# A LoRA router softmax on one Trainium2 core: sixteen idle semaphore instructions leave the programs of VectorE and ScalarE

## The chip, the core and the metric

The kernel runs on one core of a Trainium2 chip. A core has a matrix engine (TensorE, in the profile PE for the products and PEld for the loading of weights), VectorE (DVE), ScalarE (ACT), GpSimd (POOL), SyncE (SP) and 16 DMA engines. Each engine runs a program of its own, in order, and the programs meet through semaphores: an instruction may wait until a semaphore has reached a value, and may change one when it is done. A `q` behind an engine's name in the profile is its sequencer, the part that waits, branches and issues.

The metric is device time in microseconds (us). A time is a median over several runs; a profile is one execution, and its span goes from the first to the last instruction that was recorded.

## What is computed

```python
def reference(x, router_weights):          # x: 16 x 512 x 1024, router_weights: 1024 x 8, fp32
    logits = np.matmul(x, router_weights)
    exp_logits = np.exp(logits - np.max(logits, axis=-1, keepdims=True))
    return (exp_logits / np.sum(exp_logits, axis=-1, keepdims=True)).astype(np.float32)
```

There are 8,192 rows of 1,024 numbers, and a softmax over 8 router logits for each. Nearly all the data is `x`: 32 MB that are read once.

## The kernel before

The 8,192 rows are dealt to the 128 partitions, 64 to each, so that the work falls into 64 tiles (`J = 64`, numbered `j`) of 128 rows. A tile is called a row here, as in the code.

**Loading.** SP loads rows 0 to 3 in fp32 in two transfers (line 138), and ScalarE casts them to bf16 (`cast`, lines 338 to 341). The other rows are loaded by GpSimd's queue, which casts on the way: 12 transfers of four rows, three of two, five of one, and the last row in three pieces (lines 172 to 187). All are issued early, and `x_all` holds every row, so no transfer ever waits for a buffer. SP turns each landing into counts of `s_in`, one for each row (lines 156 to 162).

**The work on a row.** TensorE waits for `s_in`, turns the eight 128x128 blocks of the row (`loop_turn`, transposes into the PSUM tiles `ptv` and `pts`), VectorE copies five of the turned blocks to SBUF (`dve_copy`, line 403) and ScalarE the other three (`act_copy`, line 355), and TensorE multiplies them with the router weights (`multiply`). There are two sets of these buffers, used by even and odd rows. Two products of a constant tile (`fill`) are done in each pass of TensorE's loop besides.

**Softmax.** For eight rows at a time (`G = 8`) VectorE takes the maximum, subtracts it, sums, takes the reciprocal and scales, and ScalarE does the exponential. These steps are strung between the copies of the rows that come next.

**The loops.** TensorE, VectorE and ScalarE each run a loop with a branch at its end. VectorE's program is: two casts while it starts, a semaphore count (line 397), two register moves (lines 462 and 463), four copies for rows 0 to 3, then the body `dve_rows` (lines 469 to 488), seven times, and `dve_done` for what is left. ScalarE's is: `cast(0)`, two copies, `cast(1)`, two copies, a register move, then the body `act_rows` (lines 368 to 376), seven times, and `act_done`. The body of VectorE's loop has 20 instructions and that of ScalarE's 13, the branch included. A body handles eight rows, so the seventh pass ends with row 59. Rows 60 to 63 are handled after the loops, and row 63 in its three pieces: a maximum, an exponential and a matmul of its own for each row (`low_alone`, `power_alone`), then one sum, reciprocal and scaling for the four, and the last output transfer (line 167).

**The idle instructions.** Two constants, `DVE_IDLE, ACT_IDLE = 5, 11` (line 53), say how often a semaphore `s_idle` is raised that nobody waits for. ScalarE does it 11 times in front of `cast(0)` (lines 357 and 358), VectorE 5 times between its count of `s_p` and its register moves (lines 398 and 399). They stand ahead of the loops, each once, and so the address of everything behind them in the same program depends on them.

## Time and profile before

| | us |
|---|---|
| median of 4 runs (86.56 to 86.7) | 86.62 |
| the profiled execution, its own time | 86.61 |
| its span, first to last instruction | 85.2 |
| VectorE busy, of the span | 39.5 (46%) |
| ScalarE busy | 38.0 (45%) |
| TensorE busy (products / weight loads) | 62.6 (74%) / 51.4 (60%) |
| the queue of GpSimd's transfers, share of 16 DMA engines over the span | 90.4% |
| mean granted TensorE clock, share of full speed | 0.987 |

The profile of one execution has a page (busy times, 40 slices of the span, DMA queues, the chain of work that ended last, groups of instructions by line) and a trace behind it that can be asked for single lines, for waits or for a stretch of time. "Idle" in front of a group is time in which its engine did nothing, and the arrow names what ended it. Time of an engine that waits for data is no loss in itself; what counts is what the chain that ended last went through. Semaphore, register and branch instructions aren't counted as busy, but the trace has a record of each.

### The profile page before, as it was taken

How to read it: one execution, taken by the hardware profiler on the slowest of the kernel's cores; microseconds unless marked ns; L12 is line 12 of the kernel's file. 1: busy time of each engine (PE TensorE's matmuls, PEld its weight loads, DVE VectorE, ACT ScalarE, POOL GpSimd, SP SyncE). 2: the span in 40 equal slices, each digit the busy share in tenths (PEclk: the TensorE clock that was granted, in tenths of full speed). 3: DMA queues.
4: the chain of work that ended last, by engine and by line, in shares of the span. 5: the costliest groups of instructions: out<-in, count | busy, mean ns of one | idle time of the engine just before them, and what ended most of it. 6: DMA issues, size and time to landing. Idle time of an engine off the chain costs nothing. (4 is left out here: it accounts for less than half of the span.)

```text
span 85.2 us, 2942 instructions
## 1 busy us (share of the span) xinstructions
PE 62.6 (74%) x1094; PEld 51.4 (60%) x1094; DVE 39.5 (46%) x114; ACT 38.0 (45%) x81; POOL 13.5 (16%) x30
## 2 busy tenths in 40 slices
PE   0053849999595986949596895959598699999760
PEld 0041747878474765838475673847476588777650
DVE  0020413685274452745266362736347257665662
ACT  0039682665254352535245253525336246546470
POOL 0489999800000000000000000000000000000000
PEclk9999999999999999999999999999999999999995
DMA  2899999999999999999999999999999999999920
GB/s 46 358 427 312 223 196 227 204 227 208 223 204 223 208 223 208 227 204 227 204 227 204 227 204 227 204 223 208 223 208 204 214 215 214 203 209 211 184 102 23
DMA packets 3904, 18.12 MB, mean 213 GB/s; under 512 B 568, under 2 KB 1080, under 8 KB 2112
## 3 DMA queue, kind: packets, MB, share of 16 engines
q0 software_dynamic: 3312, 15.73, 90.4%
q1 hardware_dynamic: 576, 2.36, 7.0%
q10 hardware_dynamic: 16, 0.03, 0.3%
HBM read 33.59 MB, written 0.26 MB: 397 GB/s over the span
## 5 line engine op out<-in xcount | busy, mean ns | idle before, releaser
L355 ACT COPY xTs<-pts 128x384 bf16<-128x384 bf16 x63 | 30.0, 477 | 37.4 <-PE pts L282 37.0
L403 DVE COPY xTv<-ptv 128x640 bf16<-128x640 bf16 x63 | 31.0, 492 | 33.0 <-PE ptv L282 30.4
L282 PE MATMUL ptv<-identity,x_all 128*128 128x128 bf16 x311 | 28.3, 222 | 13.9 <-PEq L218 12.5
L282 PEld LDWEIGHTS ptv<-identity,x_all 128*128 (+1 forms) x311 | 18.5, 98 | 15.2 <-issue 15.2
L282 PE MATMUL pts<-identity,x_all 128*128 128x128 bf16 x186 | 21.1, 224 | 0.0
L269 PEld LDWEIGHTS lg<-w_bf,xTv 128*128 128x128 bf16 x305 | 15.5, 97 | 7.4 <-issue 0.6
L269 PE MATMUL spare<-filler 128*128 128x512 bf16 x61 | 19.0, 393 | 0.5
L269 PE MATMUL lg<-w_bf,xTv 128*128 128x8 bf16 x305 | 16.6, 167 | 0.0
L282 PEld LDWEIGHTS pts<-identity,x_all 128*128 x186 | 13.5, 100 | 0.0
L269 PE MATMUL lg<-w_bf,xTs 128*128 128x8 bf16 x183 | 13.2, 166 | 0.0
L174 POOL DMA_DIRECT2D x_all<-in_x_dram x20 | 10.8, 602 | 2.8 <-POOLq L151 2.8
L269 PEld LDWEIGHTS lg<-w_bf,xTs 128*128 128x128 bf16 x183 | 8.9, 96 | 0.0
L269 PEld LDWEIGHTS spare<-filler 128*128 128x128 bf16 x61 | 4.3, 99 | 2.5 <-issue 2.5
L276 PE MATMUL lg<-ident,w 8*128 8x8 f32 x8 | 1.0, 251 | 5.3 <-PEq L274 5.3
L276 PEld LDWEIGHTS lg<-ident,w 8*128 8x128 f32 x8 | 0.9, 197 | 5.3 <-issue 5.3
L341 ACT CAST x_all<-x_f 128x1024 bf16<-128x1024 f32 x4 | 4.0, 1044 | 0.0
L423 DVE TENSOR_REDUCE mx<-lg 128x8 f32 x8 | 1.8, 225 | 4.4 <-DVEq L473 3.9
L341 ACT ACT_TABLE_LOAD x1 | 1.3, 1283 | 5.7 <-ACTq L339 5.7
L392 DVE CAST identity<-ident 128x128 bf16<-128x128 f32 x1 | 0.5, 518 | 5.2 <-POOL ident L180 5.2
L344 ACT ACTIVATE ev<-ex 128x64 f32<-128x64 f32 x8 | 2.1, 257 | 1.6 <-DVE ex L423 0.9
L439 DVE TENSOR_REDUCE ssum<-ev 128x8 f32<-128x64 f32 x8 | 1.8, 221 | 0.1
L423 DVE TENSOR_TENSOR ex<-lg,mx 128x64 f32<-128x64 f32 x8 | 1.7, 216 | 0.0
(41 smaller groups left out, 16.0 us busy)
## 6 DMA issues: line engine op xcount, KB each, us to landing
x_all<-in_x_dram POOLq DMA_DIRECT2D x12, 1024.0 KB, 32.2
x_f<-in_x_dram SPq DMA_DIRECT2D x2, 1024.0 KB, 6.4
x_all<-in_x_dram POOLq DMA_DIRECT2D x3, 512.0 KB, 60.0
x_all<-in_x_dram POOLq DMA_DIRECT2D x5, 256.0 KB, 64.1
out_dram<-out_all SPq DMA_DIRECT2D x1, 208.0 KB, 1.9
x_all<-in_x_dram POOLq DMA_DIRECT2D x1, 128.0 KB, 65.7
x_all<-in_x_dram POOLq DMA_DIRECT2D x2, 64.0 KB, 65.5
out_dram<-out_all SPq DMA_DIRECT2D x1, 48.0 KB, 1.5
```

The source lines that it names most:

```text
L174: nc.gpsimd.dma_start(out=xa[:, first[i]:first[i] + r, :], in_=x_rows[:, first[i]:first[i] + r, :]).then_inc(s_ld[i], 16)
L269: return pe.matmul(spare, lhsT=filler[:, 0:P], rhs=filler, start=True, stop=True)
L276: t = pe.transpose(w_ps[:, n, :], w8[:, :, n], ident[0:KO, 0:KO])
L282: turn_like = pe.transpose(turn_ap(0, 0), xa[:, 0, 0:P], identity).ins
L341: act.copy(xa[:, k, :], x_f32[:, k, :]).then_inc(s_cast, 1)
L344: return act.activation(ev, ex, func=Exp).then_inc(s_ev, 1)
L355: act.copy(xTs[j % 2], pts[j % 2][:, 0:SN, :]).then_inc(s_c[j % 2], 1)
L392: dve.tensor_copy(out=identity, in_=ident).then_inc(s_idb, 1)
L403: dve.tensor_copy(out=xTv[j % 2], in_=ptv[j % 2][:, 0:VN, :]).then_inc(s_c[j % 2], 1)
L423: return dve.add_instruction(kind(name=f"I-{nc.next_id()}", engine=dve.engine, **k))
L439: dve.reduce_sum(ssum[:, :, 0], ev, axis=X).then_inc(s_d, 1)
```

## The change

The constants, the two loops that emit the idle instructions and the semaphore are taken out. Nothing else is edited. The semaphores that are made after `s_idle` (`s_out`, `s_st`) move down by one number. VectorE's program becomes 5 instructions shorter ahead of its loop, ScalarE's 11.

```diff
-    DVE_IDLE, ACT_IDLE = 5, 11
     VN, SN = 5, 3
...
-    s_idle = sem("s_idle")
     s_out = sem("s_out")
...
-    for _ in range(ACT_IDLE):
-        act.sem_inc(s_idle, 1)
     for i in range(2):
         cast(i)
...
     dve.sem_inc(s_p, SKIP)
-    for _ in range(DVE_IDLE):
-        dve.sem_inc(s_idle, 1)
```

## The prediction

> **What bounds the kernel now.** I read the slices of the page first, then the DMA view, the waits and the chain.

> In the slices (40 of 2.13 us each) the DMA row matters:

> ```profile
> PE   0053849999595986949596895959598699999760
> DVE  0020413685274452745266362736347257665662
> ACT  0039682665254352535245253525336246546470
> DMA  2899999999999999999999999999999999999920
> ```

> From the third slice to the 38th the DMA engines are 90% busy or more, while DVE and ACT never reach that. The DMA view for 20 to 78 us names the only traffic in that time (packets, MB, share of 16 engines):

> ```profile
> DMA packets 2335, 12.42 MB, mean 214 GB/s; under 512 B 256, under 2 KB 256, under 8 KB 1135
> q0 software_dynamic: 2335, 12.42, 104.0%
> ```

> One queue, GpSimd's loads, fills all 16 engines. The landings in the trace are correspondingly even: a transfer of four rows every 4.87 us, 1.22 us a row. The compute engines follow that stream. Who waits for whom (us in total, times, longest):

> ```profile
> ACT xTs L355 <- PE pts L282: 37.0, 54, 1.4
> DVE xTv L403 <- PE ptv L282: 30.4, 46, 2.2
> PE ptv L282 <- PEq L218: 12.5, 12, 1.4
> ...
> SPq L162 <- DMA x_all<-in_x_dram: 66.9, 20, 4.8
> ```

> DVE and ACT wait for PE, PE waits at L218 for `s_in`, which SP counts up when a transfer lands. The end is the chain of waits, from the landing of the last rows on:

> ```profile
> 80.24 0.04 issue
> 80.29 0.44 PE ptv L282 x5
> ...
> 81.60 0.18 PE extra L315 x2
> 81.79 0.18 PE lg L261 x8
> 81.97 0.09 issue
> 82.06 0.36 PE lg L329 x8
> ...
> 83.37 0.19 DVE out_all L511
> ```

> The three pieces of row 63 have their last packets in the trace at 80.3, 80.7 and 81.1 us, and PE turns the last one from 81.5. So the end is the stream's end plus a chain of short steps (to 83.56), plus the output transfer (to 85.2). DVE and ACT set the time only where they are slower than this stream, or in that last chain.

> **What the change removes, step by step.** The two rows of the idle instructions, and what follows them on their engines (the third column of a timeline row is the engine; in brackets the idle time before it):

> ```profile
> L358 ACTq EVENT_SEMAPHORE  x11: 17/17/17, 2.8 to 3.5; - x11
> 5.66 1.28 ACT L341 ACT_TABLE_LOAD   x1 [5.66 <-ACTq L339]
> L399 DVEq EVENT_SEMAPHORE  x5: 21/21/21, 6.5 to 6.9; - x5
> 9.01 0.49 DVE L403 COPY xTv<-ptv 128x640 bf16<-128x640 bf16 x1 [2.41 <-PE ptv L237]
> ```

> *ScalarE.* Eleven instructions of 17 ns each, but issued 72 to 73 ns apart in the trace (2.790 to 3.515 us). The cost is the spacing: 11 x 72.5 ns = 0.80 us. Behind them is the wait L339 for the first half of rows 0 to 3, which is passed at 5.58 us. From 3.53 to 5.58 ScalarE has nothing to do, 2.05 us; without the eleven it has 2.85 us. The work that hides them is SP's transfer, which SP issued at 0.74 us and on which nothing of ACT bears. Gain: 0. If that cover were gone, the gain would be at most 0.80 us of ScalarE's start, and still not of the stream's end.

> *VectorE.* Five, 93 ns apart: 0.46 us. They begin while the cast of the weights (6.37 to 6.60) is still running. The two register moves behind them end at 7.05, and the first copy waits for PE's first transposes until 9.01: 1.96 us of cover before, 2.42 after. Gain: 0; without cover at most 0.46 us, again ahead of a stream that does not wait for DVE.

> *Neighbours of the removed instructions.* POOL begins to issue the loads at 3.28 us, in the time of ScalarE's eleven. If semaphore writes held it up, its first two issues would be long. They took 1.20 us together, 0.60 each, where the 20 of the line have 537/600/671 ns (min/median/max). So the gain or the loss here is under 0.07 us; I take 0, because the two stand at the median. No transfer, no queue and no wait is moved or added; nobody waits for `s_idle`.

> *The addresses behind them.* VectorE's loop lies 5 instructions lower, ScalarE's 11. What that does isn't in the trace as an operation, so it needs bounds. The loops' branches:

> ```profile
> L376 ACTq COMPARE_BRANCH  x7: 40/45/50, 21.8 to 77.8; - x7
> L488 DVEq COMPARE_BRANCH  x7: 50/56/56, 21.9 to 77.9; - x7
> ```

> Seven on each engine. Were each twice as dear, it would be 7 x 45 = 0.32 us on ACT and 7 x 56 = 0.39 us on DVE, spread over 62 us in which (15.8 to 77.8) DVE is busy 32.3 us, ACT 27.1 and PE 50.9. Only the last exit stands near the end: +0.05 us. Upper end: fetching the code of a loop again is a transfer. The nearest transfers with a price from issue to landing are the output's, 1.9 and 1.5 us. Lower end: the chain that ended last holds 0.3% of "issue", 0.3% x 85.2 = 0.26 us; if addresses made all of that, it could go. Between -0.26 and +1.9 us I take 0, because in the row that would show it (the DMA view from 20 to 78 us, across six back edges) every packet is GpSimd's. The trace has a kind of packet called "instruction", six of 8,192 bytes, and all six lie before the first instruction of the span. Code that crosses no border now should cross none when it starts at the same place and ends sooner.

> [...]

> **The sum.** Span 85.2 + 0 - 0 + 0 = 85.2 us; the profiled run's own time lies 86.61 - 85.2 = 1.4 us above its span, which I leave alone: 86.6 us. The median of the runs, 86.62, is the same within 0.01.

> **The rivals.**

> *Code is fetched again at the loop's edge (slower).* Place: the exit of a loop, at 77.8 (ACT) and 77.9 us (DVE). Inside the loop such a stall is hidden as long as a pass makes up for it: a pass is eight rows at 1.22 us, 9.7 us, so the 62 us hold 6.4 passes, and PE has 62 - 50.9 = 11.1 us free in them, 1.7 us each. That is the point from which it decides. At the exit there is less. A fetch priced like an output transfer is 1.5 to 1.9 us; the copy behind DVE's branch starts at 78.24, so 0.3 us is covered, and PE's wait for row 62 (0.44 us idle at 80.29) covers as much again. That leaves 0.8 to 1.2 us, I take 1.0: 87.6 us. For it: both programs move, by different counts, and the page has no line on code. Against it: the DMA row above. Chance 0.28.

> *The loads are slowed by code traffic (slower).* If the passes fetch but stalls stay hidden, the stream pays. The plain 8,192-byte packets of SP's loads take 309 ns in the trace (median). One pair of them at each of the seven branches of both engines is 28 x 0.309 = 8.7 us of one DMA engine, or 0.54 us over 16: 87.1 us. Against it the same row. Chance 0.14.

> *A cost that stands there now goes (faster).* It can lie only in the gaps of the last chain: 0.26 us in all, 86.35 us. Against it: each "issue" piece of that chain is 0.01 to 0.09 us, like any hand-over between engines. Chance 0.16.

> *The change doesn't do what it says*, the records of L358 and L399 remaining: then nothing moves, and the time is that of the forecast.

> **How the numbers follow.** What a measurement of this kernel can tell from no change is about 0.2%, 0.17 us. No change, 86.45 to 86.8 with 86.6 as the value: 0.42. Slower by more: 0.28 + 0.14 = 0.42. Faster: 0.16. No change is the likeliest single case, so the time is 86.6. The range takes in the faster case to 86.3 (most of its 0.16), the slowed stream (87.1) and the stall at the exit up to a little over its middle, 87.9; left out is a stall that both engines pay, or one without cover (86.6 + 1.9 = 88.5), together with the far faster end some 0.15.

> **What would show it.** Right: the wait L339 still passes at 5.6 us, the first DVE copy still starts at 9.0, landings every 4.87 us, chain from 80.2, span 85.2. The rivals: "instruction" packets in the DMA view between 20 and 80 us, an "issue" or sequencer wait on DVE or ACT right behind L376 or L488, row 60's copies later than 78.24 and 78.41, or landings further apart. The forecast is wrong if any of these moves the last landing or the steps behind it by more than 0.17 us.

## The result and the profile after

The changed kernel takes 86.46 us (median; 86.36 to 86.87), the kernel before 86.6 us in the same comparison: ratio 0.9984, 95% interval 0.998 to 0.9988. That is 0.14 us, under the 0.2% that the prediction called no change, though the interval leaves 1 out.

The span did not move. It is 85.18 us in the profiled run of after and 85.17 in that of before, while the times of these two runs are 86.50 and 86.61 us. So what lies around the span went from 1.45 to 1.32 us. Each run lists its time and its span (to 0.1 us); the mean difference over the runs of after is 1.31 us. I call this the time around the span; the expectations below say "above the span".

The slices of after:

```profile
DVE  0021413267574452735266362736347257665662
ACT  0039683355554352535245253524336246545470
DMA  3899999999999999999999999999999999999920
```

The DMA engines are 90% busy or more from the third slice to the 38th, as before. The wait that covers ScalarE's eleven instructions, in the source view of after (all lines have moved up by 4 to 8), where the last two numbers are its first and last start:

```profile
L335 ACTq EVENT_SEMAPHORE  x2: 17/17/17, 5.6 to 10.2; - x2
```

The first work behind the two removed groups, in the timeline of after:

```profile
5.65 1.28 ACT L337 ACT_TABLE_LOAD   x1 [5.65 <-ACTq L335]
...
9.00 0.49 DVE L395 COPY xTv<-ptv 128x640 bf16<-128x640 bf16 x1 [2.39 <-PE ptv L233]
```

5.65 and 9.00 us stand against 5.66 and 9.01: nothing starts earlier. The DMA view of after from 20 to 78 us, then its waits:

```profile
q0 software_dynamic: 2332, 12.41, 103.9%
```

```profile
ACT xTs L351 <- PE pts L278: 37.1, 54, 1.4
DVE xTv L395 <- PE ptv L278: 29.8, 47, 2.2
PE ptv L278 <- PEq L214: 11.5, 12, 1.4
```

Again GpSimd's loads alone, in the same amount, and VectorE and ScalarE wait for TensorE, and TensorE for the landings, as before. The chain that ended last:

```profile
80.20 0.04 issue
80.24 0.44 PE ptv L278 x5
...
81.80 0.18 PE lg L257 x8
81.98 0.03 issue
82.01 0.39 PE lg L325 x8
...
83.36 0.19 DVE out_all L503
```

It starts 0.04 us earlier and ends 0.01 us earlier. Within the span the sixteen instructions were worth nothing. The experiments had to find what happens around it.

### The profile page after: what moved, and what is told of

The parts are those of the page before. It is cut to its first block, busy times and chain, and to the rows that moved or that the text cites. A ratio compares the mean times of both kernels' runs of the same rounds, so it can differ in the third digit from the quotient of the medians.

```text
span 85.2 us, 2926 instructions
## 1 busy us (share of the span) xinstructions
PE 63.8 (75%) x1094; PEld 52.2 (61%) x1094; DVE 39.5 (46%) x114; ACT 37.9 (45%) x81; POOL 13.4 (16%) x30
## 5 line engine op out<-in xcount | busy, mean ns | idle before, releaser
L278 PE MATMUL ptv<-identity,x_all 128*128 128x128 bf16 x311 | 28.8, 225 | 12.8 <-PEq L214 11.5
L265 PE MATMUL spare<-filler 128*128 128x512 bf16 x61 | 19.5, 402 | 0.5
L170 POOL DMA_DIRECT2D x_all<-in_x_dram x20 | 10.7, 615 | 2.8 <-POOLq L147 2.8
L183 POOL DMA_DIRECT2D x_all<-in_x_dram x3 | 1.8, 708 | 0.0
```

Of the source, the lines that this page charges most:

```text
L170: nc.gpsimd.dma_start(out=xa[:, first[i]:first[i] + r, :], in_=x_rows[:, first[i]:first[i] + r, :]).then_inc(s_ld[i], 16)
L183: nc.gpsimd.dma_start(out=xa[:, J - 1, c], in_=x_rows[:, J - 1, c]).then_inc(s_z[i], 16)
L265: return pe.matmul(spare, lhsT=filler[:, 0:P], rhs=filler, start=True, stop=True)
L278: turn_like = pe.transpose(turn_ap(0, 0), xa[:, 0, 0:P], identity).ins
```

## Experiments

Except for the fifth, each kernel is the kernel before with other numbers in one line; `s_idle` stays:

```diff
-    DVE_IDLE, ACT_IDLE = 5, 11
+    DVE_IDLE, ACT_IDLE = <VectorE>, <ScalarE>
```

The measured values, for each group with those of the kernel before from the same chip (mean span and mean time around the span over all runs):

```
kernel                       VectorE ScalarE  ratio   95% interval      span   around
before, chip of the first four   5     11                              85.34    1.45
  e1_dve_five_only               5      0     0.9995  0.9986-1.0004    85.26    1.50
  e2_act_eleven_only             0     11     0.9983  0.9974-0.9992    85.32    1.30
  e3_semaphore_only              0      0     0.9984  0.9975-0.9993    85.32    1.32
  e4_doubled                    10     22     0.9994  0.9985-1.0003    85.37    1.33
before, chip of the next four    5     11                              85.20    1.47
  e5_dve_five_at_end       5, at the end  0   0.9996  0.9987-1.0005    85.17    1.45
  e6_dve_ten_only               10      0     0.9987  0.9977-0.9996    85.18    1.32
  e7_act_22_only                 0     22     0.9987  0.9976-0.9998    85.22    1.32
  e8_dve_forty                  40      0     1.0010  1.0001-1.0019    85.45    1.32
before, chip of the last four    5     11                              85.30    1.46
  e9_dve_three                   3      0     1.0030  1.0018-1.0041    85.24    1.74
  e10_dve_seven                  7      0     1.0019  1.0008-1.0029    85.28    1.61
  e11_dve_twenty                20      0     0.9984  0.9975-0.9993    85.31    1.32
  e12_dve_thirty                30      0     1.0017  1.0008-1.0026    85.60    1.30
```

Within one kernel the time around the span has a standard deviation of 0.01 to 0.05 us, so that 1.3 and 1.45 are far apart. Some of it is rounding, as the spans of the runs are listed to 0.1 us. In the profiled runs, whose spans are known to the nanosecond, the time around is 1.45 us in before, 1.47 and 1.45 us with the two kernels that have five, 1.73 us with three, 1.60 us with seven, and 1.31 to 1.32 us with every other count; so the 1.50 us of e1 is not more than before.

### Whose instructions, and do they cost by number?

**e1_dve_five_only**, VectorE 5, ScalarE 0.

> VectorE's five idle instructions stay, ScalarE's eleven are gone. The changed kernel was 0.14 us faster than the kernel before, its span was the same (85.18 against 85.17 us) and its time above the span 1.32 instead of 1.45 us. Theory 1, the gain lies outside the span and belongs to ScalarE's instructions: ratio 0.9984 to the kernel before, 1.31 us above the span. Theory 2, it belongs to VectorE's: ratio 1.000, 1.41 to 1.45 us above the span. Theory 3, it goes with the number of instructions removed on either engine: 11 of 16, ratio 0.9989. Rival, the gain is inside the span: the time above the span stays at one value in all runs and the span alone moves.

**e2_act_eleven_only**, VectorE 0, ScalarE 11.

> ScalarE's eleven stay, VectorE's five are gone. Theory 1 (ScalarE's): ratio 1.000, 1.41 to 1.45 us above the span. Theory 2 (VectorE's): ratio 0.9984, 1.31 us above the span. Theory 3 (number): 5 of 16, ratio 0.9995. Rival (inside the span): time above the span as in the first kernel of this call.

**e3_semaphore_only**, both 0, the semaphore kept.

> No idle instruction, but the semaphore s_idle is still taken, so that s_out and s_st keep their numbers. If the gain comes from the semaphore (one less to keep, or the numbers behind it): ratio 1.000. If it comes from the instructions: ratio 0.9984 as in the changed kernel, 1.31 us above the span.

**e4_doubled**, VectorE 10, ScalarE 22.

> Ten idle instructions on VectorE and twenty-two on ScalarE. They are hidden by ScalarE's 2.05 us and VectorE's 1.96 us of cover (0.80 and 0.46 us more). Theory 3 (cost by number, outside the span): another 0.14 us, ratio 1.0016, 1.55 us above the span. A cost that comes in steps, at a border of the program: ratio 1.000 and 1.41 to 1.45 us above the span. Code fetched again in a loop: 'instruction' packets in the DMA view between 20 and 80 us and a ratio over 1.005.

The time around the span is 1.50 us with VectorE's five alone and 1.30 with ScalarE's eleven alone: theory 2, VectorE's. The semaphore does nothing (1.32). Doubling takes the cost away (1.33), so it isn't a price by number, and theory 3 falls. The DMA view of the doubled kernel from 80 to 85 us had something new:

```profile
q0 software_dynamic: 352, 0.18, 26.5%
q1 hardware_dynamic: 288, 0.26, 14.9%
q14 instruction: 2, 0.02, 0.8%
```

The last line is code: two packets of 8,192 bytes, fetched at 81.0 us, inside the span. In before and after there is no such line after the span's start.

### Where the loop lies, or where the program ends?

**e5_dve_five_at_end** has the five behind VectorE's last instruction.

```diff
-    DVE_IDLE, ACT_IDLE = 5, 11
+    DVE_IDLE, ACT_IDLE = 0, 0
...
     dve.tensor_tensor(
         out=outv[:, J - ALONE:J, :], in0=ev3, in1=inv3.broadcast_to([P, ALONE, N]), op=ALU.mult
     ).then_inc(s_out, 1)
+    for _ in range(5):
+        dve.sem_inc(s_idle, 1)
```

> No idle instruction ahead of the loops; VectorE's five stand behind its last instruction (line 511 in the kernel before), where they run from 83.6 us on and are over by 84.1, a microsecond before the span ends. [...] Theory 4, the 0.14 us come from where VectorE's program ends: 1.45 to 1.50 us above the span, ratio 1.000. Theory 5, they come from where its loop lies, or from five instructions run at the start: 1.31 us above the span, ratio 0.9984.

1.45 us: theory 4. VectorE's loop is where the changed kernel has it, and nothing idles at the start, and yet the 0.14 us are back. What counts is where VectorE's program ends.

**e6_dve_ten_only** and **e7_act_22_only** take the doubled kernel apart.

> Ten idle instructions on VectorE, none on ScalarE. With ten and twenty-two the time above the span was 1.33 us, with five and none 1.50. Theory 4, a step that depends on VectorE's count alone: 1.31 to 1.33 us above the span again. A count of ScalarE's that undoes VectorE's five: 1.45 us or more. The two instruction packets at 81 us in the DMA view of the doubled kernel: there again if they are VectorE's, gone if they are ScalarE's.

> Twenty-two on ScalarE, none on VectorE. Theory 4: 1.31 us above the span, ratio 0.9984, as in every kernel without VectorE's five. The two instruction packets at 81 us: there if they are ScalarE's. If they cost time at the end: span longer than that of the kernel before by more than 0.1 us.

Both have 1.32 us, and each has one of the two packets; the DMA view of ten on VectorE, 79 to 85 us, and of twenty-two on ScalarE, 20 to 85 us:

```profile
q0 software_dynamic: 490, 0.35, 38.0%
q1 hardware_dynamic: 288, 0.26, 12.4%
q14 instruction: 1, 0.01, 0.3%
```

```profile
q0 software_dynamic: 2945, 12.99, 98.1%
q1 hardware_dynamic: 288, 0.26, 1.1%
q14 instruction: 1, 0.01, 0.0%
```

### The rivals of the prediction: a border inside the loop

**e8_dve_forty**, VectorE 40.

> Forty on VectorE, none on ScalarE: 40 x 93 ns = 3.7 us, which ends at 10.2 instead of 7.0 us, so the first copy is late by some 1.2 us and the loop, with 1.7 us free in each pass, has to catch up. The prediction's rival: with VectorE's loop 35 instructions further on a border of the code may lie inside it; then instruction packets between 20 and 80 us in the DMA view, and a time of 87.1 us or more (ratio over 1.005). Without a border in it: span as before, ratio 0.998 to 1.001.

**e12_dve_thirty**, VectorE 30.

> Thirty on VectorE, none on ScalarE: 2.8 us, so the first copy is late by 0.4 us at most, against 1.2 us with forty. Theory 7 (forty's span was 0.24 us longer because of the one code packet at 22.1 us): one packet early in the stream, span again 0.2 to 0.3 us longer than the kernel before, ratio 1.000 to 1.002. Rival (forty's loss came from the late first copies): span as in the kernel before, ratio 0.9985. If each pass of the loop fetched: seven packets and over 87.1 us.

Both brought the border into VectorE's loop, and it can be seen to the instruction. The trace has the start of every sequencer instruction; the distance of two that stand next to each other in the body, in the seven passes, in ns:

```
L478 to L439   before          107 107 107 108 107 107 107
L478 to L439   e8_dve_forty    533 243 240 238 238 232 226
L485 to L486   before           96  96  96  95  96  96  96
L485 to L486   e12_dve_thirty  511 235 232 230 230 224 218
```

All other pairs of sequencer instructions at the body's end (L484 to L485, L486 to L487, L487 to L488) agree within 4 ns in the same pass. With forty the border lies in front of line 439's reduction, with thirty in front of line 486's register operation, ten instructions further on, as it must. Passing it costs 0.42 us the first time and about 0.13 us in each later pass. The back edge jumps over it every time, yet the DMA view of thirty, 20 to 78 us, has one code packet, not seven:

```profile
DMA packets 2325, 12.41 MB, mean 214 GB/s; under 512 B 256, under 2 KB 256, under 8 KB 1123
q0 software_dynamic: 2324, 12.40, 103.9%
q14 instruction: 1, 0.01, 0.0%
```

It starts at 27.12 us, 4.5 us after the border was passed at 22.62; with forty 22.14 us, 4.1 us after 18.02. VectorE went on meanwhile (with thirty its copies of that time start at 23.62, 24.75, 25.40 and 26.48 us), so the packet was not what it needed then. The loop's branch took 50 to 67 ns with thirty against 50 to 56 ns in before (line 488, seven passes), so no stall shows there. What failed is the prediction's fetch at every branch. Each crossing had its price all the same, 0.13 us; the span shows no more than the delay of the loads that is described next.

The stream, on the other hand, did lose. The landing of every second four-row transfer, earliest and latest of the 16 engines' last packets, in us:

```
                earliest / latest
before          21.86 / 22.32    31.60 / 32.05    41.33 / 41.79
e12_dve_thirty  21.90 / 22.47    31.64 / 32.51    41.37 / 42.25
```

In before both move by 9.73 to 9.74 us a step. With thirty the earliest does so too, but the latest takes 10.04 us over the step in which the packet fell, and the 0.30 us stay. The single packets show how. One of the 16 engines had ended its transfers 0.37 us behind the earliest engine; from the code packet on it ended them 0.88 us behind, while the other fifteen kept their places. It lost 0.51 us, more than the 0.32 us of the code packet, since the load's packet right behind that one took 829 ns where the others take 624. Before, it had been 0.20 us ahead of the latest engine (0.57 us behind the earliest), and so 0.30 us reached the landing. With forty one engine lost 0.50 us in the same way (from 0.14 to 0.64 us behind the earliest; 834 ns). The span is 0.30 us longer than that of the kernel before (85.60 against 85.30), with forty 0.24 us (85.45 against 85.20). The chain of thirty starts and ends later by that and by its run's scatter (80.24 and 83.37 us in before):

```profile
80.69 0.04 issue
80.74 0.44 PE ptv L282 x5
...
83.82 0.19 DVE out_all L511
```

The late first copies are not the cause: thirty has them nearly in time (9.42 against 9.01 us) and loses more than forty (10.35 us). Nor is the granted clock, 0.976 in this profile: the three runs of thirty at 1.000 have spans of 85.5 to 85.6 us. Theory 7 holds in its mechanism: one code packet made one DMA engine late, and the stream with it. Its size was met by luck, as the engine lost 0.51 us and not the packet's 0.32.

**e11_dve_twenty**, VectorE 20.

> Twenty on VectorE, none on ScalarE: 1.9 us of idle instructions, still inside the 2.42 us of cover. The border then lies some ten instructions earlier than with ten, where the packet came at 80.8 us. Theory 7: one code packet (322 ns) makes one DMA engine late by its own length, so with a packet in the full stream the last landing, and the span, is up to 0.32 us later; one packet in the span, 1.31 us above it, ratio 0.9985 to 1.002. Prediction's rival (a stall where the engine needs the block): a gap of 0.5 us or more on VectorE behind line 488's branch or in the last chain, ratio over 1.005.

The border lies ten instructions earlier than with ten, in front of row 62's copy in the last chain. The packet comes at 80.98 us, where the stream runs out, and costs nothing: span 85.31 against 85.30, ratio 0.9984, the same as the changed kernel's. No stall shows at the loop's exit: row 60's copy follows the last branch after 0.38 us (78.02 to 78.40) where before had 0.36. The border is seven instructions behind the exit here and three ahead of it with thirty; by the count below, 27 would lay it on the exit itself, and that wasn't run.

### Between none and ten

**e9_dve_three** and **e10_dve_seven**.

> Three idle instructions on VectorE, none on ScalarE. Theory 6: the 0.14 us above the span are there for a narrow set of program lengths of VectorE, where a border of the code falls on the first instructions behind the kernel's last one. With 0 it is 1.31 us above the span, with 5 it is 1.45 to 1.50, with 10 it is 1.32. Three then has either 1.31 or 1.45 us, nothing between. Rival, a cost that grows with each instruction up to some border: 1.39 us.

> Seven on VectorE, none on ScalarE. Theory 6: 1.31 or 1.45 us above the span, nothing between; with it an instruction packet inside the span if it is 1.31, as with ten. Rival (grows with each instruction up to a border): 1.50 us.

The expectation missed: neither 1.31 nor 1.45, but 1.74 and 1.61 us, and no growth with the count either. Three is 0.30% slower than the kernel before (0.18% to 0.41%), with the shortest mean span of its group: all of it is around the span. In order of VectorE's count the time around the span is 1.31 (0), 1.74 (3), 1.45 to 1.50 (5), 1.61 (7), 1.32 (10), 1.32 (20). With seven the DMA view from 85 to 90 us caught a packet that no other kernel's has:

```profile
DMA packets 1, 0.01 MB, mean 2 GB/s; under 512 B 0, under 2 KB 0, under 8 KB 0
q14 instruction: 1, 0.01, 0.6%
```

It starts at 86.50 us, 1.34 us after the span, and takes 512 ns, so that it ends 1.85 us after the span. This is code being fetched after the kernel's last instruction. That the run waited for it is not shown: the time of this run, 86.76 us, is only 1.60 us above its span, and unless that time begins later than the span does, it was over before the packet ended.

The count can be turned into a place. With thirty the border is in front of line 486, if the gap marks the place to the instruction; behind it come that instruction, two more of the body and the 17 of `dve_done`, twenty in all. So with ten the border falls right behind VectorE's last instruction, and with fewer it lies, by the count, behind the end of the kernel's program: 3 instructions behind it with seven, 5 with five, 7 with three, 10 with none. With three, five and seven the run pays 0.14 to 0.43 us; with none, where the border is 10 instructions behind the end, and with ten, where it is right at it, nothing.

## Why the prediction was right, and where it was not

**The cover of ScalarE's eleven and VectorE's five** (gain 0 each): right. The wait, the table load and the first copy stand within 0.01 us of where they were.

**The neighbours** (0, within 0.07 us): right. GpSimd's issues have a mean of 615 against 602 ns, and the landings keep their 4.87 us. But the two issues beside ScalarE's eleven did not "stand at the median": the mean of 0.60 us hides 669 and 537 ns, nearly the longest and the shortest of the 20. After has 667 and 547 ns in the same places without the eleven, so these did not make the first one long.

**The addresses within the span** (0): right, and the argument for it too. No code packet and no border came into the span, since a program that starts at the same place and ends sooner passes no new one. But "code that crosses no border now" was true of the kernel's own instructions alone. By the count above, the border lay 5 instructions behind VectorE's last one.

**"The profiled run's own time lies 1.4 us above its span, which I leave alone"**: this is the step that failed. The whole change is there: 1.45 to 1.31 us. The bounds for the addresses, -0.26 to +1.9 us, were taken from the chain and from a transfer, both inside the span. They happen to hold the -0.14 us, but for a reason that the text didn't have. It is luck, too, that 86.46 us still lies in the 86.45 to 86.8 us of "no change": nothing in the text said why the time around the span should stay.

**The faster rival** (the gaps of the last chain, 0.26 us): right in sign, wrong in place. The chain's gaps are 0.18 instead of 0.24 us, but two groups of products beside them took 0.09 us longer (lines 311 and 325 of after), and the chain ends within 0.01 us of where it did.

**The stall at the loop's exit** (1.0 us): did not come with a border seven instructions behind the exit (e11) or three ahead of it (e12). A border in the loop's body costs 0.42 us once and 0.13 us in each later pass, less than the 1.7 us that the prediction found free in a pass.

**The stream slowed by code** (0.54 us): the mechanism is real, and both terms of its price were wrong. No run shows a pair of packets at each branch: with thirty and with forty there is one packet in all, not 28. And its time wasn't spread over 16 engines: it fell to one, and the load waited for that one. In before SP counted each of the twelve four-row loads 0.37 us after the last of the 16 engines had closed it. One packet of 322 ns made its engine 0.51 us later, and of that 0.30 us reached the span.

**Two readings of the page** were wrong without bearing on the sum: ScalarE does reach 90%, in the fourth slice, while it starts (table load and casts), and TensorE turns the last piece of row 63 from 81.60 us (`extra`); at 81.5 us it is the second piece.

Shown: the cost belongs to VectorE, lies around the span, depends on where its program ends, and is gone when the border, by the gaps and the count, is inside the kernel, right at its end or 10 instructions behind it. Shown once, with seven: a code packet behind the span. Only argued: that the 0.14 us of the kernel before have to do with such a packet, since its trace has none there; and a wait for the packet's end does not fit the one that was seen. So by what way the place of the border costs time stays open, and with it what lies behind the end of VectorE's program, why a border 10 instructions behind it is free, and why three costs more than seven. ScalarE's counts between 0, 11 and 22 weren't tried, nor VectorE's 1, 2, 4, 6, 8 and 9.

None of the twelve has a ratio clearly better than the changed kernel's 0.9984; the best is 0.9983. Ten, twenty or none on VectorE are alike within their intervals, and none is the simplest.

## What to carry to other kernels

The time of a run has a part around the span, and a change that leaves every row of the trace alone can still move it: compare both the span and the time above it before looking for a cause in the trace. The length of an engine's program is a quantity of its own, which decides where a border of its code falls (ten idle instructions fewer moved it ten instructions on); seven instructions behind the kernel's last one, by the count, it was worth 0.43 us here, so an edit that shifts a program by a few instructions wants a second length beside it before a difference of some tenths of a per cent is put down to what the edit does. With the DMA engines 80% busy or more in every slice from 20 to 78 us (thirty and forty), a single foreign packet delayed the one engine that it fell to, and the load with it: 322 ns of code cost an engine 0.50 to 0.51 us and the span 0.24 to 0.30 us, not a sixteenth of 0.32.

## What was not expected of the hardware

In the full stream the code packet came 4.1 to 4.5 us after the border was passed, and the engine had gone on without it. Both times it ran between the last data packet of a four-row load on its DMA engine and the 4-byte packet that closes that load (22 ns in before, where each load has 16 of them), so it came at the end of a load and not behind the whole queue of loads. With ten on VectorE the packet starts at 80.78 us, though the border lies behind line 511, which runs at 83.29; row 62's copy starts at 80.65 and is ten instructions in front of the border. So the packet was fetched at least nine instructions ahead of what the engine did. With twenty the border is ten instructions nearer, but the packet came no earlier (80.98 us), so a packet's start doesn't tell when it was asked for.
